# Gate and up projections of a decoder step on one NeuronCore: the normed tokens, the last splits and one weight sum in another place

## The chip, the cores and the metric

The kernel runs on one core of one Trainium2 chip. The metric is the device time of one execution in microseconds (us). Three runs of the kernel before took 882.13, 884.52 and 888.44 us, median 884.52. The profiled execution took 884.46 us.

## The reference, cut to what matters

One layer of a decoder for 512 prompt tokens and 8 sample tokens, width 1024. The part in question is its dense feed-forward network, in float32, at the end of the layer:

```python
hf = rmsnorm(x, g_ffn)
x = x + (jax.nn.silu(hf @ w_gate) * (hf @ w_up)) @ w_down      # 1024 -> 2816 -> 1024
```

Behind it only one more norm follows.

## The kernel before, in words

Tokens lie along the free dimension: all 520 of them, as two halves of `H2` = 260 columns, and features on the 128 partitions. Every float32 operand is split in two reduced parts, a rounded one (`hi`, a cast on ScalarE) and the rest (`lo`, a subtraction on VectorE, lines 191 and 192 for activations and Strassen weights, 208 and 209 for plain weights). A product is three matmuls: hi x hi, hi x lo, lo x hi.

**The feed-forward network** has 22 blocks `f` of 128 hidden features. The first four (`PLAIN`) are computed plainly: `proj` (line 223) multiplies the gate's weights and then the up weights with A, the split of the tokens with their gain but without the inverse norm `r_bc`; VectorE reads the PSUM (`pfg` at line 1194, `pfu` at 1200), multiplying by `r_bc`. PSUM for these has two buffers.

The other 18 blocks compute gate and up together by a Strassen-Winograd scheme: the 2 x 2 blocks are gate and up against the two halves of the features for the weights (a11, a12 in the raw tile `g`; a21, a22 in `u`), and the two halves of the features against the two halves of the tokens for the activations. Seven products `j` of 12 matmuls (84 for a block) replace eight. Three more weight operands, s1 = a21 + a22, s2 = s1 - a11, s4 = a12 - s2, and s3 = a11 - a21, are sums that VectorE makes (lines 1175 to 1178) for block f+1 while block f is multiplied; s3 and s1 share a tile, and these tiles have two buffers, the same that plain weights use. Raw weight tiles have three. The split weight operands (`qhi`, `qlo`) rotate through eight buffers.

The seven activation operands `xs` are made once. `operands()` multiplies X by gain and `r_bc` (line 1152, eight instructions, 'normed tokens'), forms four sums (1156 to 1164) and splits seven times. It is a generator: `spawn` puts it among the tasks and `step()` asks each task for its next piece. The results of products are read from PSUM at lines 1221 to 1232 in an order set by `j`; line 1234 writes the block's product to `FR`.

**The down projection** (line 1257) needs the 22 blocks split. Blocks 0 to 7 go to A during the Strassen stage (`ff_split`). Blocks 8 to 21 go to `TT`, where `xs` lies: products of the last block free it, two blocks' worth for each product. It takes the two PSUM buffers that `pfa` and `pfb` have had.

**The order of the work** on each engine is made when the program is built: a list scheduler with a model of the machine's times (`schedule_with_timeline_sim=True`) takes the instructions in the order in which the code issues them as priority and sets them as they come ready in its model. Each engine then works its list strictly in order. Weight loads are issued on SP's queue (`wraw`, line 199); POOL's queue issues nothing in this part of the kernel before.

Of the kernel before, what the change touches and what calls it, by code (L numbers as in the profile page):

```python
# [13 lines left out]
AF = mybir.ActivationFunctionType  # L14
# [9 lines left out]
P = 128  # L24
D = 1024
KB = 8
# [114 lines left out]
def decoder_step(ctx: ExitStack, tc: tile.TileContext, i: dict, o: list):  # L141
# [23 lines left out]
    def ps1(name):  # L165
        return psums[-1].tile([P, 512], F32, tag="msc", name=name)
# [30 lines left out]
    def wraw(at, n):  # L197
        raw = wp.tile([P, KB * P], F32, tag="wraw", name="wraw", bufs=3)
        sp.dma_start(raw[:, :n], i["weights"][at : at + P * n].rearrange("(p n) -> p n", p=P))
        return raw  # L200
# [29 lines left out]
    def spawn(gen, group=None):  # L230
        tasks.append([gen, 0, group])
# [914 lines left out]
    def xsplit(j, x):  # L1146
        split(*xs[j], x)

    def operands():

        for k in range(KB):
            dve.scalar_tensor_tensor(xn[:, :, k], halves(X[:, k]), vec[:, k, V_GF : V_GF + 1], r_h, ALU.mult, ALU.mult)
            if k % 2:
                yield 1
        b11, b21, b12, b22 = (xn[:, a, k : k + 4].rearrange("p k n -> p (k n)") for a in range(2) for k in (0, 4))
        t3 = fr[:, 12 * N : 14 * N]
        dve.tensor_tensor(t3, b22, b12, ALU.subtract)
        dve.tensor_tensor(b12, b12, b11, ALU.subtract)
        xsplit(0, b11)
        yield 1  # L1160
        dve.tensor_tensor(b11, b22, b12, ALU.subtract)
        xsplit(4, b21)
        yield 1
        dve.tensor_tensor(b21, b21, b11, ALU.subtract)
        for j, x in ((1, t3), (6, b22), (3, b12), (2, b11), (5, b21)):
            xsplit(j, x)
            yield 1

    def weight_operands(out):

        g, u = (wraw(W.next()[1], KB * P) for _ in range(2))
        yield 1
        s13, s24 = (wp.tile([P, KB * P], F32R, tag=t, name="wsum", bufs=2).bitcast(F32) for t in ("whi", "wlo"))
        a11, a12, a21, a22, s3, s1, s2, s4 = (t[:, z : z + 4 * P] for t in (g, u, s13, s24) for z in (0, 4 * P))
        dve.tensor_tensor(s3, a11, a21, ALU.subtract)  # L1175
        dve.tensor_tensor(s1, a21, a22, ALU.add)
        dve.tensor_tensor(s2, s1, a11, ALU.subtract)
        dve.tensor_tensor(s4, a12, s2, ALU.subtract)
        for w in (a11, s3, s2, s1, a12, a22, s4):
            hi, lo = (tp.tile([P, 4 * P], F32R, tag="q" + t, name="q" + t, bufs=8) for t in ("hi", "lo"))  # L1180
            split(hi, lo, w)
            out.append((hi, lo))
            yield 1

    def ff_split(f, raw):
        split(ff(0, f, slice(None)), ff(1, f, slice(None)), raw)

    spawn(operands())
    ops = []
    for f in range(PLAIN):  # L1190
        ps = proj(A, "pfg")
        gu = tp.tile([P, 4, H2], F32, tag="gu", name="gu").rearrange("p (a z) n -> p a (z n)", a=2)
        g, u = gu[:, 0], gu[:, 1]
        dve.tensor_tensor(halves(g), ps[:, :, :H2], r_h, ALU.mult)
        act.activation(g, g, AF.Silu)
        if f == PLAIN - 1:
            spawn(weight_operands(ops))
        step()
        ps = proj(A, "pfu", ahead=int(f < PLAIN - 1))
        dve.tensor_tensor(halves(u), ps[:, :, :H2], r_h, ALU.mult)  # L1200
        dve.tensor_tensor(FR[:, f], u, g, ALU.mult)
        step()
    drain()
    for f in range(PLAIN, FB):
        last, nxt = f == FB - 1, []
        more = weight_operands(nxt) if not last else iter(())
        next(more, None)
        ab, cd = ps2("pfa"), ps2("pfb")
        ps = [*(ps1(z)[:, :H2] for z in ("pfc", "pfd")), ab[:, 0, :H2], ab[:, 1, :H2], ps1("pfe")[:, :H2], cd[:, 0, :H2], cd[:, 1, :H2]]
        gu = tp.tile([P, 4, H2], F32, tag="gu", name="gu")  # L1210
        g1, g2, v1, v2 = (gu[:, z] for z in range(4))
        for j, (out, (wh, wl), (xh, xl)) in enumerate(zip(ps, ops, xs)):
            for k in range(4):
                for w, x in ((wh, xh), (wh, xl), (wl, xh)):
                    pe.matmul(  # L1215
                        out, w[:, k * P : (k + 1) * P], x[:, k * H2 : (k + 1) * H2],
                        start=k == 0 and w is wh and x is xh, stop=k == 3 and w is wl,
                    )
            next(more, None)
            if j == 0:  # L1220
                act.copy(g1, out)
            elif j == 2:
                dve.tensor_tensor(g2, out, g1, ALU.add)
                dve.tensor_tensor(v1, ps[1], g2, ALU.add)
            elif j == 3:
                dve.tensor_tensor(gu[:, 1::2], out.unsqueeze(1).broadcast_to([P, 2, H2]), gu[:, 1:3], ALU.add)  # L1226
            elif j == 4:
                dve.tensor_tensor(g1, out, g1, ALU.add)
                act.activation(g1, g1, AF.Silu)
            elif j == 6:  # L1230
                dve.tensor_tensor(gu[:, 1:3], cd[:, ::-1, :H2], gu[:, 1:3], ALU.add)
                act.activation(g2, g2, AF.Silu)
                to = FR[:, f - KB if f >= KB else f]
                dve.tensor_tensor(halves(to), gu[:, 0:2], gu[:, 2:4], ALU.mult)
            if f - PLAIN < KB and j == 5:
                ff_split(f - PLAIN, FR[:, f - PLAIN])
            if last:
                if j == 1:
                    W.fill(1)
                for z in (2 * j, 2 * j + 1):  # L1240
                    ff_split(KB + z, FR[:, z])
        list(more)
        ops = nxt
    tp_cm.__exit__(None, None, None)
# [4 lines left out]
    for obs in ((0, 1), *((ob,) for ob in range(2, KB - 1))):  # L1249
        pss = [ps2("pfd") for _ in obs]  # L1250
        for k0 in range(0, FB, KB):
            for ps in pss:
                hi, lo = W.get()
                for k in range(k0, min(k0 + KB, FB)):
                    for w, s in ((hi, 0), (hi, 1), (lo, 0)):
                        for a in range(2):
                            pe.matmul(  # L1257
                                ps[:, a, :H2], w[:, k - k0], ff(s, k, slice(a * H2, (a + 1) * H2)),
                                start=k == 0 and w is hi and s == 0, stop=k == FB - 1 and w is lo,
                            )  # L1260
        for ob, ps in zip(obs, pss):
            xb = X[:, ob]
            dve.tensor_tensor(halves(xb), halves(xb), ps[:, :, :H2], ALU.add)
            square(yp, ob)
            act.activation(xb, xb, AF.Copy, scale=vec[:, ob, V_GO : V_GO + 1])
# [106 lines left out]
```

## Time and profile before

| what | value |
|---|---|
| median of three runs | 884.52 us |
| the profiled execution | 884.46 us |
| its span on the core | 882.7 us |
| PE busy in the span | 838.9 us (95%) |
| mean granted TensorE clock | 0.983 |
| plain blocks of the feed-forward network | from 495 to 550 us |
| Strassen blocks | from 550 to 734 us |
| down projection | from 740 us |

The span is the time from the first to the last instruction; what lies around it is 1.8 us. PE is TensorE, DVE VectorE, ACT ScalarE, POOL GpSimd, SP the queue that issues loads. L1152 is line 1152 of the kernel. A wait is put down to the instruction that ended it.

### The profile page before, as it was taken

The page shows a single profiled execution, that of the slowest core. Times are in us where ns is not written, and L with a number is a line of the kernel's source. Part 1 is how long each engine was busy: PE and PEld are TensorE (multiplying, and loading weights), DVE is VectorE, ACT ScalarE, POOL GpSimd, SP SyncE. Part 2 cuts the span into 40 slices and gives each one's busy share as a digit, 9 for nine tenths or more (in the row PEclk, how much of TensorE's full clock was granted, in tenths as well). Part 3 has the DMA queues.
Part 4 walks back from the last instruction along what each step waited for, and adds up shares of the span by engine and source line. Part 5 has one row for each costly group of instructions (what it writes and reads, how often), then busy time and mean ns, then how long its engine had stood idle before and what let it go on. Part 6 is the DMA issues. An engine that isn't in the chain of part 4 may idle for free.

```text
span 882.7 us, 16987 instructions
## 1 busy us (share of the span) xinstructions
PE 838.9 (95%) x6707; PEld 821.9 (93%) x6707; DVE 673.3 (76%) x1509; ACT 397.4 (45%) x791; POOL 182.4 (21%) x188
## 2 busy tenths in 40 slices
PE   6999999999999999999999889999999997999994
PEld 5989989999999999889999879999999997999994
DVE  5899999877786678867888897999999997222224
ACT  5455435444546354355443554554445554222221
POOL 5544432221024301424323300000000000010011
PEclk9999999999999999999999989999999998999997
DMA  8333223334235336784764112223332232233213
GB/s 270 98 97 124 83 96 121 123 100 133 94 144 195 118 129 217 254 283 135 223 215 133 66 66 73 97 96 115 122 101 96 97 120 66 84 105 94 90 43 98
DMA packets 34600, 110.56 MB, mean 125 GB/s; under 512 B 4000, under 2 KB 8480, under 8 KB 34264
## 3 DMA queue, kind: packets, MB, share of 16 engines
q1 hardware_dynamic: 28752, 96.06, 33.9%
q0 software_dynamic: 3616, 12.34, 3.9%
q10 hardware_dynamic: 2152, 1.08, 0.5%
q8 instruction: 53, 0.87, 0.4%
q14 instruction: 27, 0.22, 0.1%
HBM read 100.38 MB, written 9.07 MB: 124 GB/s over the span
## 4 chain that ended last, share of the span: by engine, by line
PE 76%; DVE 15%; DMA 3%; issue 2%; ACT 2%; POOL 1%; SPq 0%; DVEq 0%; ACTq 0%; POOLq 0%
PE pfd L1257 13%; PE pfa L1215 6%; PE pfb L1215 6%; PE pcq L223 5%; PE pgt L223 4%; PE pwc L223 4%; PE ppl L223 4%; PE pfg L223 3%; PE pfc L1215 3%; PE pwo L223 3%; PE pfe L1215 3%; PE prp L223 3%; PE pfd L1215 3%; PE pfu L223 2%; DVE cv L518 2%
## 5 line engine op out<-in xcount | busy, mean ns | idle before, releaser
L208 ACT CAST whi<-wraw 128x1024 fp32r<-128x1024 f32 (+1 forms) x104 | 107.2, 1032 | 185.4 <-PE pfd L1257 69.6
L209 DVE TENSOR_TENSOR wlo<-wraw,whi 128x1024 fp32r<-128x1024 f32 (+1 forms) x85 | 108.9, 1282 | 74.9 <-ACT whi L208 72.9
L302 POOL TENSOR_TENSOR ssq<-ssq,sq 128x520 f32<-128x520 f32 x18 | 29.3, 1628 | 371.8 <-ACT sq L301 366.6
L191 ACT CAST qhi<-wsum 128x512 fp32r<-128x512 f32 x72 | 42.9, 619 | 54.1 <-DVE wsum L1175 45.7
L1257 PE MATMUL pfd<-TT,whi 128*128 128x260 f32 x392 | 62.8, 282 | 0.0
L209 POOL TENSOR_TENSOR wlo<-wraw,whi 128x1024 fp32r<-128x1024 f32 x19 | 46.0, 2419 | 67.7 <-ACT whi L208 62.6
L1215 PE MATMUL pfa<-TT,qhi 128*128 128x260 f32 x288 | 53.8, 284 | 0.0
L1257 PEld LDWEIGHTS pfd<-TT,whi 128*128 128x128 f32 x392 | 53.7, 188 | 0.0
L1215 PE MATMUL pfb<-TT,qhi 128*128 128x260 f32 x288 | 53.0, 283 | 0.0
L192 DVE TENSOR_TENSOR qlo<-wsum,qhi 128x512 fp32r<-128x512 f32 x72 | 47.9, 687 | 0.0
L223 PE MATMUL pwc<-B,whi 128*128 128x260 f32 x256 | 43.8, 287 | 3.6 <-DVE X L291 3.0
L223 PE MATMUL ppl<-A,whi 128*128 128x260 f32 x256 | 46.4, 295 | 0.6 <-DVE up L510 0.6
L223 PE MATMUL pcv<-A,whi 128*128 128x260 f32 x256 | 45.6, 294 | 1.1 <-ACT whi L208 1.1
L1215 PEld LDWEIGHTS pfb<-TT,qhi 128*128 128x128 f32 x288 | 44.5, 188 | 0.0
L1215 PEld LDWEIGHTS pfa<-TT,qhi 128*128 128x128 f32 x288 | 44.4, 188 | 0.0
L223 PE MATMUL pgt<-A,whi 128*128 128x260 f32 x256 | 44.0, 287 | 0.0
L223 PE MATMUL prp<-A,whi 128*128 128x260 f32 x256 | 43.8, 287 | 0.0
L1257 PE MATMUL pfd<-A,whi 128*128 128x260 f32 x224 | 37.3, 290 | 6.0 <-DVE gu L1226 6.0
L223 PE MATMUL pcq<-A,whi 128*128 128x260 f32 x256 | 42.0, 283 | 0.0
L1215 PE MATMUL pfa<-TT,qlo 128*128 128x260 f32 x144 | 40.9, 284 | 0.6 <-DVE qlo L192 0.6
L223 PE MATMUL pwo<-B,whi 128*128 128x260 f32 x256 | 41.3, 283 | 0.0
L1215 PE MATMUL pfb<-TT,qlo 128*128 128x260 f32 x144 | 40.8, 283 | 0.0
(435 smaller groups left out, 2625.4 us busy)
## 6 DMA issues: line engine op xcount, KB each, us to landing
wraw<-in_weights_dram SPq DMA_DIRECT2D x132, 512.0 KB, 3.7
kv<-in_cache_k_dram SPq DMA_DIRECT2D x16, 512.0 KB, 4.3
kv<-in_cache_v_dram SPq DMA_DIRECT2D x16, 512.0 KB, 4.3
wraw<-in_weights_dram SPq DMA_DIRECT2D x8, 384.0 KB, 3.1
X<-in_x_dram SPq DMA_DIRECT2D x2, 1040.0 KB, 6.0
Cs<-in_state_C_dram POOLq DMA_DIRECT2D x4, 512.0 KB, 5.1
out_dram<-Cs POOLq DMA_DIRECT2D x4, 512.0 KB, 3.4
Ss<-in_state_S_dram POOLq DMA_DIRECT2D x4, 512.0 KB, 3.9
```

The lines of the kernel that those rows point to most:

```text
L191: act.copy(hi, src)
L192: dve.tensor_tensor(lo, src, hi.bitcast(F32), ALU.subtract)
L208: act.copy(hi[:, :n], raw[:, :n])
L209: (pool if index in LO_ON_POOL else dve).tensor_tensor(lo[:, :n], raw[:, :n], hi[:, :n].bitcast(F32), ALU.subtract)
L223: pe.matmul(ps[:m, a, :H2], w[:, k, c0 : c0 + m], x[:, s, xk, a * H2 : (a + 1) * H2], start=first and w is hi and s == 0, stop=last and w ...
L302: (dve if ob == KB - 1 else pool).tensor_tensor(ssq, ssq, s, ALU.add)
L518: dve.scalar_tensor_tensor(cv[:, :LO], up[:, j : j + LO], wc(j), cv[:, :LO], ALU.mult, ALU.add)
L1215: pe.matmul(out, w[:, k * P : (k + 1) * P], x[:, k * H2 : (k + 1) * H2], start=k == 0 and w is wh and x is xh, stop=k == 3 and w is wl,)
L1257: pe.matmul(ps[:, a, :H2], w[:, k - k0], ff(s, k, slice(a * H2, (a + 1) * H2)), start=k == 0 and w is hi and s == 0, stop=k == FB - 1 and ...
```

## The change

Three edits. (1) `spawn(operands())` stands behind the issue of the first gate block's reading instead of ahead of the plain blocks. (2) The seven products come in another order (operands a11, a12, s3, s2, s1, a22, s4), PSUM readings are put together differently, and the splits of blocks 8 to 21 are asked for from the fifth product of the last block on, two per product, and then one per two steps of the down projection. (3) s1 isn't summed by VectorE: a21 is loaded a second time into the place of s1 by a plain DMA on SP's queue, and a22 is loaded onto it by a DMA on POOL's queue that adds.

```diff
@@ -1159,24 +1159,28 @@
         xsplit(0, b11)
         yield 1
         dve.tensor_tensor(b11, b22, b12, ALU.subtract)
-        xsplit(4, b21)
+        xsplit(1, b21)
         yield 1
         dve.tensor_tensor(b21, b21, b11, ALU.subtract)
-        for j, x in ((1, t3), (6, b22), (3, b12), (2, b11), (5, b21)):
+        for j, x in ((2, t3), (3, b11), (4, b12), (5, b21), (6, b22)):
             xsplit(j, x)
             yield 1
 
     def weight_operands(out):
 
-        g, u = (wraw(W.next()[1], KB * P) for _ in range(2))
-        yield 1
+        at, at_u = W.next()[1], W.next()[1]
+        g, u = wraw(at, KB * P), wraw(at_u, KB * P)
         s13, s24 = (wp.tile([P, KB * P], F32R, tag=t, name="wsum", bufs=2).bitcast(F32) for t in ("whi", "wlo"))
         a11, a12, a21, a22, s3, s1, s2, s4 = (t[:, z : z + 4 * P] for t in (g, u, s13, s24) for z in (0, 4 * P))
+        for z, op in ((0, ALU.bypass), (4 * P, ALU.add)):
+            (pool if z else sp).dma_start(
+                s1, i["weights"][at_u : at_u + P * KB * P].rearrange("(p n) -> p n", p=P)[:, z : z + 4 * P], accum_op=op
+            )
+        yield 1
         dve.tensor_tensor(s3, a11, a21, ALU.subtract)
-        dve.tensor_tensor(s1, a21, a22, ALU.add)
         dve.tensor_tensor(s2, s1, a11, ALU.subtract)
         dve.tensor_tensor(s4, a12, s2, ALU.subtract)
-        for w in (a11, s3, s2, s1, a12, a22, s4):
+        for w in (a11, a12, s3, s2, s1, a22, s4):
             hi, lo = (tp.tile([P, 4 * P], F32R, tag="q" + t, name="q" + t, bufs=8) for t in ("hi", "lo"))
             split(hi, lo, w)
             out.append((hi, lo))
@@ -1185,7 +1189,13 @@
     def ff_split(f, raw):
         split(ff(0, f, slice(None)), ff(1, f, slice(None)), raw)
 
-    spawn(operands())
+    unsplit = list(range(KB, FB))
+
+    def rest_split(n):
+        for _ in range(min(n, len(unsplit))):
+            f = unsplit.pop(0)
+            ff_split(f, FR[:, f - KB])
+
     ops = []
     for f in range(PLAIN):
         ps = proj(A, "pfg")
@@ -1193,6 +1203,8 @@
         g, u = gu[:, 0], gu[:, 1]
         dve.tensor_tensor(halves(g), ps[:, :, :H2], r_h, ALU.mult)
         act.activation(g, g, AF.Silu)
+        if f == 0:
+            spawn(operands())
         if f == PLAIN - 1:
             spawn(weight_operands(ops))
         step()
@@ -1206,7 +1218,8 @@
         more = weight_operands(nxt) if not last else iter(())
         next(more, None)
         ab, cd = ps2("pfa"), ps2("pfb")
-        ps = [*(ps1(z)[:, :H2] for z in ("pfc", "pfd")), ab[:, 0, :H2], ab[:, 1, :H2], ps1("pfe")[:, :H2], cd[:, 0, :H2], cd[:, 1, :H2]]
+        pc, pd, pe_ = (ps1(z)[:, :H2] for z in ("pfc", "pfd", "pfe"))
+        ps = [pc, pd, ab[:, 0, :H2], ab[:, 1, :H2], pe_, cd[:, 0, :H2], cd[:, 1, :H2]]
         gu = tp.tile([P, 4, H2], F32, tag="gu", name="gu")
         g1, g2, v1, v2 = (gu[:, z] for z in range(4))
         for j, (out, (wh, wl), (xh, xl)) in enumerate(zip(ps, ops, xs)):
@@ -1218,15 +1231,15 @@
                     )
             next(more, None)
             if j == 0:
-                act.copy(g1, out)
-            elif j == 2:
-                dve.tensor_tensor(g2, out, g1, ALU.add)
-                dve.tensor_tensor(v1, ps[1], g2, ALU.add)
+                act.copy(g2, out)
+            elif j == 1:
+                dve.tensor_tensor(g1, out, g2, ALU.add)
+                act.activation(g1, g1, AF.Silu)
             elif j == 3:
+                dve.tensor_tensor(g2, out, g2, ALU.add)
+                dve.tensor_tensor(v1, ps[2], g2, ALU.add)
+            elif j == 4:
                 dve.tensor_tensor(gu[:, 1::2], out.unsqueeze(1).broadcast_to([P, 2, H2]), gu[:, 1:3], ALU.add)
-            elif j == 4:
-                dve.tensor_tensor(g1, out, g1, ALU.add)
-                act.activation(g1, g1, AF.Silu)
             elif j == 6:
                 dve.tensor_tensor(gu[:, 1:3], cd[:, ::-1, :H2], gu[:, 1:3], ALU.add)
                 act.activation(g2, g2, AF.Silu)
@@ -1235,10 +1248,10 @@
             if f - PLAIN < KB and j == 5:
                 ff_split(f - PLAIN, FR[:, f - PLAIN])
             if last:
-                if j == 1:
+                if j == 3:
                     W.fill(1)
-                for z in (2 * j, 2 * j + 1):
-                    ff_split(KB + z, FR[:, z])
+                if j > 3:
+                    rest_split(2)
         list(more)
         ops = nxt
     tp_cm.__exit__(None, None, None)
@@ -1258,6 +1271,8 @@
                                 ps[:, a, :H2], w[:, k - k0], ff(s, k, slice(a * H2, (a + 1) * H2)),
                                 start=k == 0 and w is hi and s == 0, stop=k == FB - 1 and w is lo,
                             )
+                    if k % 2:
+                        rest_split(1)
         for ob, ps in zip(obs, pss):
             xb = X[:, ob]
             dve.tensor_tensor(halves(xb), halves(xb), ps[:, :, :H2], ALU.add)
```

In the listings that follow, names stand as in the code: `FR` and `X` hold tokens, `gu` the readings, `TT` the split operands and later the split blocks.

VectorE where the plain blocks begin; a leading minus marks rows of before alone, a plus rows of the change alone:

```order
 L278 SCALAR_TENSOR_TENSOR r_bc<-r_bc,nrml 128x260 x2
-L1152 SCALAR_TENSOR_TENSOR FR<-X,vec,r_bc 128x2x260 x6
-L1194 TENSOR_TENSOR gu<-pfg,r_bc 128x520
-L1152 SCALAR_TENSOR_TENSOR FR<-X,vec,r_bc 128x2x260 x2
-L1200 TENSOR_TENSOR gu<-pfu,r_bc 128x520
+L1204 TENSOR_TENSOR gu<-pfg,r_bc 128x520
+L1152 SCALAR_TENSOR_TENSOR FR<-X,vec,r_bc 128x2x260 x8
+L1212 TENSOR_TENSOR gu<-pfu,r_bc 128x520
 L209 TENSOR_TENSOR wlo<-wraw,whi 128x1024
 L192 TENSOR_TENSOR TT<-FR,TT 128x1040
```

The reading of the first gate block moved ahead of all eight instructions for the normed tokens; the reading of the first up block and a weight split stay behind them.

VectorE of the change in one of the last Strassen blocks, with numbers that tell buffers apart: `wsum_8790`, `wsum_8928` and `wsum_9066` are the tiles of s3 and s1 of three blocks that follow each other (the third uses the first one's buffer):

```order
L192 TENSOR_TENSOR qlo_8885<-wsum_8790,qhi_8884 128x512
L1240 TENSOR_TENSOR gu_8799<-pfa_8794,gu_8799 128x260
L192 TENSOR_TENSOR qlo_8902<-wraw_8788,qhi_8901 128x512
L1242 TENSOR_TENSOR gu_8799<-pfe_8798,gu_8799 128x2x260
L192 TENSOR_TENSOR qlo_8918<-wsum_8791,qhi_8917 128x512
L1244 TENSOR_TENSOR gu_8799<-pfb_8795,gu_8799 128x520
L192 TENSOR_TENSOR qlo_8954<-wraw_8924,qhi_8953 128x512
L1247 TENSOR_TENSOR FR_6315<-gu_8799 128x520
L192 TENSOR_TENSOR qlo_8971<-wraw_8924,qhi_8970 128x512
L1181 TENSOR_TENSOR wsum_9067<-wsum_9066,wraw_9062 128x512
L1236 TENSOR_TENSOR gu_8937<-pfd_8935,gu_8937 128x260
L192 TENSOR_TENSOR qlo_8989<-wsum_8928,qhi_8988 128x512
```

The first row is the split of s1 of one block, which frees its buffer; L1181 reads the s1 that the two loads have put there for the block after next, eight rows later. In before no row of VectorE waits for a load of s1; its sum stood at line 1176.

VectorE of the change in the last block:

```order
L1236 TENSOR_TENSOR gu<-pfd,gu 128x260
L192 TENSOR_TENSOR TT<-FR,TT 128x520 x3
L1239 TENSOR_TENSOR gu<-pfa,gu 128x260
L192 TENSOR_TENSOR TT<-FR,TT 128x520
L1240 TENSOR_TENSOR gu<-pfa,gu 128x260
L192 TENSOR_TENSOR TT<-FR,TT 128x520 x2
L1242 TENSOR_TENSOR gu<-pfe,gu 128x2x260
L192 TENSOR_TENSOR TT<-FR,TT 128x520 x4
L1244 TENSOR_TENSOR gu<-pfb,gu 128x520
```

In before, eight splits and the readings of `pfd` and `pfe` stood between the block's first reading of `pfa` (L1223) and its second one (L1226), and three of the splits directly ahead of that; now both readings of `pfa` follow that of `pfd` with three splits and one split between.

## Rows read from the trace of the kernel before

**Rows 1.** The page, part 1: busy us (share of span) x instructions.

```profile
PE 838.9 (95%) x6707; PEld 821.9 (93%) x6707; DVE 673.3 (76%) x1509; ACT 397.4 (45%) x791; POOL 182.4 (21%) x188
```

**Rows 2.** Stages: length, busy us per engine, granted clock, DMA share, GB/s.

```profile
495.00:498.50 3.50, 3.50 (x19) 3.50 (x18) 3.50 (x4) 3.03 (x5) 3.12 (x2) 0.54 0.02 5
...
509.00:513.40 4.40, 0.01 (x1) 0.02 (x1) 4.40 (x8) 1.97 (x3) 0.00 (x0) 0.83 0.00 1
513.40:518.70 5.30, 5.29 (x24) 5.30 (x25) 5.30 (x7) 3.79 (x5) 0.00 (x0) 0.50 0.22 79
...
553.00:720.00 167.00, 167.00 (x1389) 166.98 (x1388) 159.32 (x283) 82.55 (x165) 0.00 (x0) 1.00 0.32 107
...
734.50:740.50 6.00, 0.01 (x1) 0.00 (x0) 5.97 (x11) 1.30 (x3) 0.00 (x0) 0.72 0.19 66
740.50:744.30 3.80, 3.77 (x18) 3.80 (x19) 2.02 (x3) 2.33 (x3) 0.00 (x0) 0.54 0.02 4
744.30:760.00 15.70, 15.70 (x133) 15.70 (x132) 2.45 (x2) 2.72 (x3) 0.00 (x0) 1.00 0.20 59
```

**Rows 3.** PE's waits from 480 us on: in total us, times, longest.

```profile
PE pfd L1257 <- DVE gu L1226: 6.0, 1, 6.0
PE pfg L223 <- DVE gu L1194: 4.4, 1, 4.4
PE pwc L223 <- DVE X L291: 3.0, 2, 2.7
...
PE pfa L1215 <- DVE qlo L192: 0.6, 1, 0.6
PE pfe L1215 <- ACT qhi L191: 0.5, 1, 0.5
```

**Rows 4.** VectorE in order of time, first gate and up block: start, us.

```profile
508.55 4.11 DVE L1152 SCALAR_TENSOR_TENSOR FR<-X,vec,r_bc 128x520 f32<-128x520 f32 x6
512.58 0.69 DVE L1194 TENSOR_TENSOR gu<-pfg,r_bc 128x520 f32<-128x520 f32 x1
513.18 1.42 DVE L1152 SCALAR_TENSOR_TENSOR FR<-X,vec,r_bc 128x520 f32<-128x520 f32 x2
```

**Rows 5.** PE in order of time at the same place.

```profile
513.41 1.21 PE L223 MATMUL pfg<-A,whi 128*128 128x260 f32 x4 [4.41 <-DVE gu L1194]
```

**Rows 6.** VectorE in order of time, end of the last block.

```profile
737.19 0.43 DVE L1224 TENSOR_TENSOR gu<-pfd,gu 128x260 f32<-128x260 f32 x1
737.52 0.42 DVE L1228 TENSOR_TENSOR gu<-pfe,gu 128x260 f32<-128x260 f32 x1
737.86 1.92 DVE L192 TENSOR_TENSOR TT<-FR,TT 128x520 fp32r<-128x520 f32 x3
739.69 0.70 DVE L1226 TENSOR_TENSOR gu<-pfa,gu 128x520 f32<-128x520 f32 x1
```

**Rows 7.** VectorE's groups in the Strassen stage: x count | busy, mean ns.

```profile
L1176 DVE TENSOR_TENSOR wsum<-wraw 128x512 f32<-128x512 f32 x16 | 11.0, 685 | 0.0
```

**Rows 8.** VectorE in order of time, one block inside that stage.

```profile
694.04 1.28 DVE L192 TENSOR_TENSOR qlo<-wsum,qhi 128x512 fp32r<-128x512 f32 x2
```

**Rows 9.** DMA issues of the whole run: KB each, median us from issue to landing.

```profile
wraw<-in_weights_dram SPq DMA_DIRECT2D x132, 512.0 KB, 3.7
...
wraw<-in_weights_dram SPq DMA_DIRECT2D x8, 384.0 KB, 3.1
...
Cs<-in_state_C_dram POOLq DMA_DIRECT2D x4, 512.0 KB, 5.1
...
Ss<-in_state_S_dram POOLq DMA_DIRECT2D x4, 512.0 KB, 3.9
...
mraw<-in_mem_dram POOLq DMA_DIRECT2D x2, 512.0 KB, 7.0
...
cosr<-in_rope_dram POOLq DMA_DIRECT2D x1, 260.0 KB, 2.9
```

**Rows 10.** The same view of 560 to 720 us alone.

```profile
wraw<-in_weights_dram SPq DMA_DIRECT2D x32, 512.0 KB, 4.3
```

## The prediction

> **What bounds the kernel now.** I read busy shares first, then stages, then what the busiest engine waits for. PE is busy 95% of the span [rows 1]. In the table of stages [rows 2] the Strassen stage (553 to 720 us) has PE at 167.00 of 167 us at full granted clock, with VectorE at 159.32: nothing done for another engine can gain there while PE stays full; it can only cost. So the gain must lie at the two edges. Before it, 509 to 513.4 us, PE does nothing and VectorE all the time; behind it, 734.5 to 740.5 us, the same. After each gap the granted clock is about half for a while. PE's waits [rows 3] name four: 4.4 us on the reading of the first gate block, 6.0 us on a reading of the last block, 0.6 and 0.5 us on splits. The profiled execution took 884.46 us around a span of 882.7 us, as good as the median of 884.52; the sum is made against 884.46.
>
> **The start.** VectorE has the inverse norms at 508.55 us and then forms six normed token blocks before it reads the gate block [rows 4]; PE, which has two PSUM buffers there, stands until that reading ends [rows 5]. In the change the reading comes first and all eight follow. It then ends at 508.55 + 0.69 = 509.2; from a reading's end to PE's start the rows show 513.41 - (512.58 + 0.69) = 0.14 us, so PE starts at 509.4 instead of 513.41: 4.0 us saved. The 24 matmuls behind the gap took 5.30 us at clock 0.50 (the 1.2 GHz level); at full clock one costs 167.00 / 1389 = 0.120 us, so 2.9 us: 2.4 saved if the clock stays up. Against that: the eight normed blocks (4.11 + 1.42 us) now stand ahead of the reading of the first up block and of the split of the weights of the second up block. PE reaches that block at 509.4 + 48 x 0.120 = 515.2; the reading is over at 509.2 + 5.4 + 0.6 = 515.2, just in time, but the split ends at 516.3 where PE wants it four matmuls in, at 515.7: 0.6 to 0.7 us lost. Net 5.7 us. Some matmuls of the first Strassen block now stand inside the plain ones; moving them is free by the same addition: the buffer of their weights is free at 527.3 us (the split of the third up block), a load lands 3.7 to 4.3 us later [rows 9, 10], the cast adds 0.6, which is 532.2 at the latest, and PE arrives at 533.2.
>
> **The end.** In the last block VectorE has three splits directly ahead of the reading of pfa [rows 6]; PE needs that PSUM for the down projection and waits 6.02 us. In the change VectorE's order from the end of product pfd on is: its reading, three splits, a reading of pfa, one split, the other reading of pfa; that is 3 x 0.34 + 4 x 0.6 = 3.4 us, while PE has five more products (60 x 0.120 = 7.2 us) before the down projection. So I cost this wait at nothing: 6.0 saved. 18 matmuls then took 3.80 us at clock 0.54 instead of 2.2: 1.6. The waits of 0.6 and 0.5 us inside the block come from splits queued ahead of its operands [rows 3, 6], which now come later: 1.1. The splits moved into the down projection are hidden: VectorE is busy 2.45 of 15.7 us there [rows 2], and their readers come after 16 steps of six matmuls, 11.5 us. Sum 8.7 us; both edges 14.4.
>
> **The adding loads.** Removed: one VectorE sum of 128x512 per block, 18 in all. A run of two such operations costs 1.28 us, so 0.6 each in a row [rows 7, 8]: VectorE has some 11 us less, all beside PE, worth nothing by itself. The different order of the readings is worth nothing either, with the same six per block. Added per block: a plain 256 KB load on SP's queue and a 256 KB adding one on POOL's, which waits for the first. POOL has no other work there. The order table shows the new chain: the buffer of block k's sum is free when its split is done; then plain load, then adding load, then VectorE's L1181 of block k+2, and VectorE runs in order, so from there everything waits for it, among it the next block's split of its sum. One pass of this loop is c (both loads with their hand-overs) plus VectorE's work from L1181 to that split. I counted that work over the 16 steps with 0.6 us per 512-column operation and reading, 0.34 per 260-column one (737.19 to 737.52 in [rows 6]): it runs from 0 to 5.2 us, 4.3 in each of the last three, 51.0 in all. PE needs 84 x 0.120 = 10.1 us a block, 161.6 for 16. The loop holds PE up once 16 c + 51.0 > 161.6: **from c = 6.9 us on, 16 us for each further us.** Short lags are covered by VectorE's lead; I give no credit for it.
>
> No trace shows an adding load. The plain load: 384 KB take 3.1 us and 512 KB 3.7 [rows 9], thus 2.5 to 3.0 for 256 KB, I take 2.8. The adding one: at least a plain POOL load of its size, 2.9 (260 KB, cosr); at most the slowest POOL load of 512 KB, 7.0. To add, the old 256 KB must be fetched besides the new, so the nearest rows are POOL's loads of 512 KB: 3.9 and 5.1; I take 3.9, since here nothing else is on POOL. Three hand-overs of 0.14 make 0.4. c = 2.8 + 3.9 + 0.4 = 7.1 us: 16 x 7.1 + 51.0 - 161.6 = 3.0 us lost. With the ends 2.5 + 2.9 and 3.0 + 7.0 c is 5.8 (no loss) to 10.4 (56 us).
>
> The Trainium skill (DMA: Bandwidth & Descriptors, Anatomy of one DMA) prices a POOL load at 2.0 us plus bytes by 436 GB/s: an estimate of 2.6 us for 256 KB and 3.2 for twice that, so c of 5.6 to 6.2 and no loss; the rows, 2.9 for 260 KB and 3.9 for 512 KB, stand above it. The same page (Rules for kernel authors) says that an accumulating load reads its destination and writes it later, and needs a wait for the earlier load; no run here shows it yet, and it speaks for the doubled bytes.
>
> **Forecast.** 884.46 - 14.4 + 3.0 = **873 us**, chance 0.46; its own range 870 to 876.
>
> **Rivals.**
> *The loads are cheap* (0.10): c stays under 6.9, as the 2.9 us of cosr allow; nothing is lost and 870 us result. For it: POOL's queue is empty. Against: the table's larger loads. The skill's formula above is this rival's rule.
>
> *The loads share the engines* (0.20): two weight loads per block go on beside them. 512 KB take 4.3 us in this stage against 3.7 over the whole run [rows 9, 10]; 0.6 us more on one of the two gives c = 7.7, 12.6 us lost, 882.7 us, no change. That the queues of SP, ACT and POOL end in the same 16 engines is also what the skill states (the same page, Issuing engines are not separate DMA queues).
>
> *Slower: the adding load sets the pace* (0.16): it takes 5.1 us, as the POOL loads of Cs do, and the plain one 3.4. Then c = 8.9, 16 x 8.9 + 51.0 - 161.6 = 31.8 us lost, 902 us; PE would wait 2 us in every block, on splits behind L1181. The point where the gain is eaten is c = 6.9 + 14.4/16 = 7.8. For it: POOL loads of 512 KB spread from 3.9 to 7.0 us. Against: those ran beside POOL's own work.
>
> *The edges give less* (0.08): the waits go but the clock falls all the same (it was 0.54 at 495 us too, behind a wait of 2.7 us [rows 2, 3]), or the last readings wait for a weight split put ahead of them; 4 us less, 877 us. That the change does not do what it says I exclude: the order shows the reading ahead of all normed tokens, 18 adding loads, and each reading between splits.
>
> **Numbers.** A measurement tells about 1%, 8.8 us, from no change. Faster by more (under 875.7) needs c under 7.3 with full edges: the forecast but a tail, and the cheap loads, 0.54. Same: the shared engines, less gain, the tail, 0.29. Slower: 0.17. The range 868 to 893 leaves out the slow adding load and a thin end below.
>
> **What would show it.** The start: PE's idle time before the second gate block under 0.5 us, clock 1.00 behind it, and a wait of some 0.7 us in the second up block. The end: no wait of the first pfd on VectorE. The loop: landing time of the wsum loads, 2.8 and 3.9 us, and VectorE's idle time before L1181; if that sums to more than some 10 us and PE has idle time in 553 to 720 us, the loop binds. Wrong would be: an adding load over 5 us, or new PE waits on the casts of the first Strassen block.

## The result, and the profile after

The changed kernel takes **905.99 us** (median of four runs, 903.52 to 909.44) where the kernel before takes 885.43 beside it: ratio 1.024, 95% interval 1.0205 to 1.0274. It is slower, by about 20 us; the forecast was 873, its range 868 to 893. The profiled execution took 909.44 us around a span of 907.6; it is the slowest of the four, so the table below, made of profiled executions, shows a loss of 24.9 us where the medians show 20.6.

Three stretches of PE's work tell where the time is. They run from the first gate matmul to the first down matmul (gate and up), from there to the last down matmul, and from that to the end of the span. The third kernel is the best of the experiments (e14); its profiled execution is the fastest of its six, and 4.0 us of its lead lie ahead of the first gate matmul, where nothing was changed.

| | before | changed | e14 |
|---|---|---|---|
| first gate matmul starts, us | 495.05 | 494.02 | 491.05 |
| gate and up, us | 245.5 | 265.4 | 234.3 |
| down products, us | 129.0 | 127.5 | 127.5 |
| behind the last down matmul, us | 13.1 | 20.7 | 13.5 |

So the changed kernel lost 19.9 us in gate and up and 7.6 behind the last matmul, and won 1.5 in the down products; 1.0 us lies ahead of everything that was changed.

**The start went as predicted.** The first two fences are VectorE and PE of the changed kernel in order of time, to be held against [rows 4] and [rows 5] (start, us, and in brackets the wait); the third is the table of stages that answers to [rows 2].

```profile
507.59 0.70 DVE L1204 TENSOR_TENSOR gu<-pfg,r_bc 128x520 f32<-128x520 f32 x1
508.21 5.45 DVE L1152 SCALAR_TENSOR_TENSOR FR<-X,vec,r_bc 128x520 f32<-128x520 f32 x8
```

```profile
508.44 0.71 PE L223 MATMUL pfg<-A,whi 128*128 128x260 f32 x4 [0.38 <-DVE gu L1204]
```

```profile
509.00:513.40 4.40, 4.40 (x39) 4.40 (x38) 4.40 (x7) 2.91 (x3) 0.00 (x0) 1.00 0.00 0
513.40:518.70 5.30, 4.98 (x40) 4.62 (x39) 5.30 (x7) 3.94 (x4) 0.00 (x0) 1.00 0.34 99
```

The wait is 0.38 us instead of 4.41, and the granted clock stays at 1.00 where it was 0.83 and 0.50. **The wait at the end went too.** The first down matmul waits 0.87 us, not 6.0 [rows 3]; what took it away is the subject of e10:

```profile
759.39 0.75 PE L1270 MATMUL pfd<-A,whi 128*128 128x260 f32 x4 [0.87 <-DVE gu L1240]
```

**Between the edges PE is now held up.** First PE's waits from 545 to 755 us (total, times, longest), then the same stretch in the table of stages:

```profile
PE pfa L1228 <- DVE gu L1240: 15.5, 9, 3.2
PE pfb L1228 <- DVE gu L1244: 1.8, 1, 1.8
PE pfc L1228 <- ACT gu L1234: 1.7, 1, 1.7
PE pfc L1228 <- DVE qlo L192: 1.1, 2, 0.9
PE pfa L1228 <- ACT qhi L191: 0.2, 1, 0.2
```

```profile
545.00:755.00 210.00, 189.70 (x1478) 186.16 (x1477) 162.68 (x288) 94.57 (x187) 14.83 (x17) 0.96 0.51 137
```

The waits sum to 20.3 us, which is the idle time of that row (210 - 189.70). And 1478 matmuls at 0.120 us would be 177.4 us, not 189.70. Of these 12 us some 8 are the clock, which falls after several of the waits (0.96 in the mean, and 0.04 x 210 = 8.4); the rest is not taken apart. PE waits for VectorE's readings of PSUM, but VectorE itself waits for the weight sum. Line L1181 (min, median and max ns, first and last start) and what its engine sat idle for (us, times), then the two loads of the sum (KB, median us to landing), then one block's loads and L1181 on SP, POOL and VectorE:

```profile
L1181 DVE TENSOR_TENSOR wsum<-wsum,wraw x18: 684/693/695, 547.2 to 736.1; 128x512 f32<-128x512 f32 x18
...
  DMA wsum<-in_weights_dram: 45.5, 15
```

```profile
wsum<-in_weights_dram SPq DMA_DIRECT2D x18, 256.0 KB, 2.7
wsum<-in_weights_dram POOLq DMA_DIRECT2D x18, 256.0 KB, 4.8
```

```profile
716.67 0.33 SPq L1176 DMA_DIRECT2D wsum<-in_weights_dram  x1
...
728.62 0.33 SPq L1176 DMA_DIRECT2D wsum<-in_weights_dram  x1
```

```profile
719.89 0.87 POOL L1176 DMA_DIRECT2D wsum<-in_weights_dram  x1 [11.63 <-DVE gu L1244]
```

```profile
724.21 0.69 DVE L1181 TENSOR_TENSOR wsum<-wsum,wraw 128x512 f32<-128x512 f32 x1 [3.01 <-DMA wsum<-in_weights_dram]
```

One pass of the loop can be read off: plain load issued at 716.67, adding load 3.2 us later, L1181 4.3 us behind that, and 4.4 us of VectorE's work until the next plain load goes out at 728.62: 11.95 us for a block of which PE needs 10.1. (What ended POOL's wait is, by the code, the landing of the plain load, 0.56 us ahead, and not the VectorE reading that the bracket names.) Over the last 16 blocks the two loads took 8.72 us in the mean (3.63 from issue to issue, 5.09 from the adding load's issue to L1181) and VectorE's work 2.60; the sum, 11.32, is the mean distance of two L1181, by the way it is counted.

**Behind the last matmul stands what the prediction did not have.** ScalarE at the end of the last block, and then in the last 26 us:

```profile
755.24 1.28 ACT L1258 ACT_TABLE_LOAD   x1
756.53 0.63 ACT L191 CAST TT<-FR 128x520 fp32r<-128x520 f32 x1
757.18 1.28 ACT L1237 ACT_TABLE_LOAD   x1
758.48 0.42 ACT L1237 ACTIVATE gu<-gu 128x260 f32<-128x260 f32 x1
...
882.37 1.28 ACT L273 ACT_TABLE_LOAD   x1 [2.47 <-PE pn L1292]
...
884.16 1.28 ACT L275 ACT_TABLE_LOAD   x1
...
891.59 1.28 ACT L273 ACT_TABLE_LOAD   x1
892.88 0.37 ACT L273 ACTIVATE nrml<-pn,vec 128x130 f32<-128x130 f32 x1
893.27 1.28 ACT L275 ACT_TABLE_LOAD   x1
...
894.89 1.28 ACT L273 ACT_TABLE_LOAD   x1
...
896.57 1.28 ACT L275 ACT_TABLE_LOAD   x1
```

The same place of the kernel before, where one load, behind the last Silu, serves all that follows:

```profile
742.99 1.28 ACT L1245 ACT_TABLE_LOAD   x1
...
871.60 0.35 ACT L273 ACTIVATE nrml<-pn,vec 128x130 f32<-128x130 f32 x1
871.98 0.31 ACT L275 ACTIVATE nrml<-nrml 128x130 f32<-128x130 f32 x1
872.20 0.35 ACT L273 ACTIVATE nrml<-pn,vec 128x130 f32<-128x130 f32 x1
872.58 0.31 ACT L275 ACTIVATE nrml<-nrml 128x130 f32<-128x130 f32 x1
```

The set of logarithm and exponential is asked for by a line that is pinned behind the ScalarE instruction written just ahead of it. Before, that was the split of the last block's own result, which cannot run before the last Silu. The change writes the split of an older block there, whose data lie ready; so the set is loaded at 755.24, ahead of the last block's two Silu, the Silu at 758.48 fetches its own set back, and at the end logarithm and exponential fetch a set for each call: six loads of 1.28 us. Four of them stand one behind the other on the last chain (5.1 us). The two at 882.37 and 884.16, for the first half of the tokens, hold up VectorE, so that the square of the last tokens starts 3.6 us behind the last down matmul instead of 1.0 (2.5 us); together that is the 7.6 us of the table. That logarithm and exponential can share one set is what the Trainium skill states (ScalarE: Activation LUTs, Table sets: the hidden batching unit); the trace of before agrees, in which the four calls follow each other without a load. The same page (What ACT_TABLE_LOAD costs) adds a drain of 1.38 us to each switch; no such gap is seen here (a load ends at 892.87, the next ACTIVATE starts at 892.88).

### The profile page after: what moved, and what is told of

The parts are those of the page before. It is cut to its first block, busy times and chain, and to the rows that moved or that the text cites. A ratio compares the mean times of both kernels' runs of the same rounds, so it can differ in the third digit from the quotient of the medians.

```text
span 907.6 us, 17189 instructions
## 1 busy us (share of the span) xinstructions
PE 846.2 (93%) x6707; PEld 825.6 (91%) x6707; DVE 662.1 (73%) x1491; ACT 406.9 (45%) x798; POOL 198.2 (22%) x206
## 4 chain that ended last, share of the span: by engine, by line
PE 58%; DVE 20%; DMA 12%; issue 5%; ACT 3%; POOL 1%; SPq 0%; DVEq 0%; POOLq 0%; ACTq 0%
PE pfd L1270 12%; DMA wsum<-in_weights_dram 7%; PE pcq L223 5%; PE pgt L223 4%; PE ppl L223 3%; PE pwc L223 3%; PE pwo L223 3%; PE prp L223 3%; PE pfa L1228 3%; PE pfb L1228 3%; DVE qlo L192 2%; PE pfg L223 2%; DVE wlo L209 2%; DVE cv L518 2%; PE pfu L223 1%
## 5 line engine op out<-in xcount | busy, mean ns | idle before, releaser
L1228 PE MATMUL pfa<-TT,qhi 128*128 128x260 f32 x288 | 58.5, 303 | 15.7 <-DVE gu L1240 15.5
L1228 PEld LDWEIGHTS pfa<-TT,qhi 128*128 128x128 f32 x288 | 48.3, 205 | 17.8 <-DVE gu L1240 6.7
L1176 POOL DMA_DIRECT2D wsum<-in_weights_dram x18 | 15.8, 876 | 219.7 <-DVE gu L1244 45.1
L1181 DVE TENSOR_TENSOR wsum<-wsum,wraw 128x512 f32<-128x512 f32 x18 | 12.5, 692 | 47.6 <-DMA wsum<-in_weights_dram 45.5
L1228 PE MATMUL pfa<-TT,qlo 128*128 128x260 f32 x144 | 42.8, 297 | 0.0
```

Source lines behind the costliest of these rows:

```text
L1176: (pool if z else sp).dma_start(s1, i["weights"][at_u : at_u + P * KB * P].rearrange("(p n) -> p n", p=P)[:, z : z + 4 * P], accum_op=op)
L1228: pe.matmul(out, w[:, k * P : (k + 1) * P], x[:, k * H2 : (k + 1) * H2], start=k == 0 and w is wh and x is xh, stop=k == 3 and w is wl,)
```

## The experiments

Ratios are against the kernel before, in the same group of runs, with 95% intervals.

**The table set (e1), the sum given back to VectorE (e2), both (e3), the loads alone (e4).**

```diff
 e1, on the changed kernel
                 act.activation(g2, g2, AF.Silu)
+                if last:
+                    tc.keep_in_program_order(act.preload_act_table_set(LOG_EXP))
...
     tp_cm.__exit__(None, None, None)
-    tc.keep_in_program_order(act.preload_act_table_set(LOG_EXP))
 e2, on the changed kernel
-        for z, op in ((0, ALU.bypass), (4 * P, ALU.add)):
-            (pool if z else sp).dma_start(
...
+        dve.tensor_tensor(s1, a21, a22, ALU.add)
         dve.tensor_tensor(s2, s1, a11, ALU.subtract)
```

e1: 

> The changed kernel with one thing moved: the load of the log/exp table set stands right behind the last Silu instead of behind the last split that is written. Theory (table set): in the changed kernel that load slid ahead of the last block's two Silu, which brought their own set back, so that six set loads of 1.28 us stand in the last 25 us of the program, and from the last down matmul to the end it takes 20.6 us instead of 13.0. Then this kernel has one such load behind the last Silu, 13 us behind the last down matmul and about 898.4 us in all (906.0 less 7.6). Rival (the end is long for another reason, the clock or the output's transfers): 906 within 2 us.

e2: 

> The changed kernel without its adding loads: VectorE adds the weight halves again as in the kernel before; the two moves of splits and the new order of products stay. Theory (loads): the weight loads cost all of the loss in the middle of the gate and up stage, about 33 us, so 873 to 878 us (884.5 less 14.4 for the two edges, plus up to 7.6 while the table set is loaded too early). Rival (the new order of products and of the VectorE's PSUM reads holds TensorE): PE still waits 10 us or more for VectorE between 560 and 740, and the time stays above 890.

e3 (e1 and e2 together): 

> Both: VectorE adds, and the table set is loaded behind the last Silu. Loads and table set: 870 us (884.5 less 14.4), 7 to 8 us under the kernel with the sum alone. If the table set is off the path: the same as that kernel within 2 us. If the order of products is the loss: above 885.

e4 (the loads written into the kernel before): 

> The kernel before with the adding loads alone: old order of splits and of products, last splits where they were. Theory (loads, in any order of the products): about 33 us slower than before, 912 to 920. Rival 1 (the loop of loads as the prediction had it, with 4.8 instead of 3.9 us for the adding load, 8.0 us in all): 17 us slower, 902. Rival 2 (only in the new order does the wait stand ahead of PSUM reads): within 5 us of before.

Measured: e1 909.14 us (1.0284, 1.0243 to 1.0325); e2 881.32 (0.9964, 0.9943 to 0.9985); e3 874.75 (0.9879, 0.9834 to 0.9925); e4 901.91 (1.0205, 1.0162 to 1.0248).

e2 settles the main point: without the adding loads, and with everything else of the change, PE waits between the edges for 2.4 us in the last block and for little else (0.2 us), and 25 us of the 906 are gone. The view is that of PE's waits again:

```profile
PE pfb L1225 <- DVE gu L1241: 2.4, 1, 2.4
```

Still e2 lies 3.3 us above the range expected of it, and e3 4.8 us above its 870: the edges give less than 14.4. e3 against e2 prices the table set: 6.6 us, and the stretch behind the last matmul is 13.3 us instead of 21.2. e4 came out at rival 1's 902, so the loads cost in either order of the products. But its own loop is short: the two loads take 8.57 us, VectorE's work 1.96, and L1181 stand 10.52 us apart, which over 16 blocks is 6.7 us more than PE's 10.1. Gate and up is 14.8 us longer than before, and 10.5 of that lie between the last L1181 and the first down matmul; PE's waits from 545 to 750 us, most of them on readings of pfa, sum to 12.1 us. The hit is in the figure, not in the whole of its reasoning. e1 missed its 898: its end is 13.6 us long, as expected, but its gate and up stage is 270.9 us. I come back to that with e13.

**Is it the adding (e5), is it the loop (e6, e9)?** Three kernels on top of e1.

```diff
 e5
-        for z, op in ((0, ALU.bypass), (4 * P, ALU.add)):
+        for z, op in ((0, ALU.bypass), (4 * P, ALU.bypass)):
 e6
...
+        n = next(blocks)
+        if n > 1:
+            s1 = FR[:, 8 + n % 6, : 4 * P]
         for z, op in ((0, ALU.bypass), (4 * P, ALU.add)):
-            (pool if z else sp).dma_start(
+            tc.keep_in_program_order((pool if z else sp).dma_start(
...
 e9, on e6
-        g, u = wraw(at, KB * P), wraw(at_u, KB * P)
         s13, s24 = (...)
...
         for z, op in ((0, ALU.bypass), (4 * P, ALU.add)):
...
+        g, u = wraw(at, KB * P), wraw(at_u, KB * P)
```

e5: 

> The changed kernel with the table set behind the last Silu, whose second load of each block overwrites the weight sum instead of adding to it (the sum is then one half of the weights, and the outputs are another function): same loads, same bytes, same waits, without the adding. Theory (loop of two tiles: both loads, then VectorE's work up to the split that frees the tile, 8.7 + 2.6 = 11.3 us a block against 10.1 of TensorE): a plain second load lands about 1.9 us sooner, the loop takes 9.4 us, TensorE's 10.1 us decide again, and only the later first operand is left of the loss: 880 us, 878 to 886. Rival (the two more loads a block cost by sharing the DMA engines with the weights, or by a wait ahead of PSUM reads whatever its length): above 895.

e6: 

> The changed kernel with the table set behind the last Silu and, from the third block on, the weight sum in six places that are free in the token buffer, so that the first load waits for no split; it is issued right behind the load of its up weights. The adding loads stay. Theory (loop of two tiles): with the loop open the loads' 8.7 us lie beside TensorE's work, and what is left is the later first operand: 883 us, 879 to 888. Rival (the adding load's length itself, or the new order of products, holds TensorE): above 895, VectorE still waiting 2 us or more a block for the sum.

e9: 

> The kernel with the six places in the token buffer, and both loads of the sum now asked for ahead of the block's gate and up loads instead of behind them. In the kernel with the places alone the loop had only closed elsewhere: the up load waited in SP's queue until s4, which stands behind the wait for the sum, had read the gate tile (L1187 ends at 664.74, base load 665.20), and a block took 11.4 us as before. Theory (what costs is a loop through the two loads, whichever tile closes it): now the first load goes out about a block earlier, VectorE no longer waits for the sum, a block takes TensorE's 10.1 us, and the time is 877 to 886. Rival (long adding loads or the new order of products hold TensorE without a loop): above 893, VectorE still waiting 1 us or more a block for the sum.

Measured: e5 886.59 us (1.0031, 1.0005 to 1.0056); e6 901.66 (1.0198, 1.0161 to 1.0236); e9 884.93 (1.0012, 0.9988 to 1.0037).

e5: a plain second load lands in 3.6 us where the adding one takes 4.8. The two lines are the loads of e5; the third is what VectorE sat idle for ahead of L1181:

```profile
wsum<-in_weights_dram SPq DMA_DIRECT2D x18, 256.0 KB, 2.8
wsum<-in_weights_dram POOLq DMA_DIRECT2D x18, 256.0 KB, 3.6
```

```profile
  DMA wsum<-in_weights_dram: 26.1, 15
```

The loop is 7.36 + 2.70 = 10.06 us, the distance of two L1181 is 10.06, and 21 to 23 us of the time of e1 and e13 are gone. The estimate was 1.9 us for the adding, it is 1.2. e5 came out 6.6 us above what I expected: with the loop as long as its own block PE still waits 11.3 us from 545 to 745 us, 3.2 of them ahead of the down products.

e6 failed, and told more than a hit would have. The sum had six places and its first load waited for no split, and still VectorE waited for the sum in each block. VectorE, then SP, in order of time:

```profile
662.51 0.69 DVE L1186 TENSOR_TENSOR wsum<-FR,wraw 128x512 f32<-128x512 f32 x1 [2.53 <-DMA FR<-in_weights_dram]
...
664.06 0.68 DVE L1187 TENSOR_TENSOR wsum<-wraw,wsum 128x512 f32<-128x512 f32 x1
```

```profile
664.82 0.33 SPq L199 DMA_DIRECT2D wraw<-in_weights_dram  x1
665.20 0.42 SPq L1181 DMA_DIRECT2D FR<-in_weights_dram  x1
```

L1187 (s4) is the last reader of a weight tile; when it ends, at 664.74, SP's next weight load may go, and the sum's first load stands behind that in SP's queue. The loop had closed through another tile: 8.84 + 2.54 = 11.38 us a block. In e9 the sum's loads stand ahead of the block's weight loads, and PE is idle for only 2.5 us of 168 (573 to 741 us):

```profile
573.00:741.00 168.00, 165.45 (x1368) 164.70 (x1367) 148.95 (x264) 88.97 (x174) 12.23 (x14) 1.00 0.57 152
```

1368 matmuls in 165.45 us are 0.121 us each, at full clock, though the adding loads are all there. So it is neither the adding itself nor the new order of products that holds PE, but a loop that is longer than PE's block. In that stretch VectorE still sits idle 3.2 us ahead of L1187 for the sum and 11.2 for weights that are now asked for later, nearly all of it off PE's path. e9 lacks 10 us to e3. PE's waits from 545 to 746 us sum to 9.9 us in e9 (3.1 at 567.6 us, 4.1 ahead of the down products) and to 3.7 in e3; the rest is not taken apart.

**Which edge brings what (e8, e10, e11, e14).** On the kernel before: e8 has the first edit alone; e10 has the late splits of the second edit, but the old order of products and readings, with the table set placed as in e1; e11 has both. e14 is e3 again, with more executions.

```diff
 e8
-    spawn(operands())
...
         act.activation(g, g, AF.Silu)
+        if f == 0:
+            spawn(operands())
 e10
             if last:
...
-                for z in (2 * j, 2 * j + 1):
-                    ff_split(KB + z, FR[:, z])
+                if j > 3:
+                    rest_split(2)
...
+                    if k % 2:
+                        rest_split(1)
```

e8: 

> The kernel before with the first edit alone: the normed tokens are asked for behind the first plain block's reading. Theory (the start edge as the prediction has it): 5.7 us less than before, 879.4. Rival (the wait only moves to a later split of the tokens): within 2 us of before.

e10: 

> The kernel before with the second edit alone (last splits behind the last block's readings), and the table set loaded behind the last Silu. Theory (the end edge as the prediction has it): 8.7 us less than before, 875.2 to 876.4. Rival (splits that are now made beside the down products hold TensorE there): within 3 us of before, with waits for TT in the down products.

e11: 

> The kernel before with both edges, the table set behind the last Silu, the old order of products and VectorE's own sum. Theory (the two edges add up, the new order of products has no part in them): 884.5 less 14.4, 870, within 3 us of the kernel with the new order and the sum (874.75). Rival (the new order is needed for the end edge): 878 or more.

e14: 

> The changed kernel with VectorE's sum and the table set behind the last Silu, again: 874.75 us within 2, some 7 us under the kernel with both edges in the old order of products (881.8), if the new order of products is what lets the last block's readings stand ahead of the splits.

Measured: e8 881.07 us (0.9966, 0.9939 to 0.9993); e10 885.06 (1.0005, 0.9979 to 1.0031); e11 881.78 (0.9948, 0.9926 to 0.9970); e14 **872.50** (0.9853, 0.9823 to 0.9884).

e10 is the surprise: the late splits alone give nothing. VectorE and PE at the end of its last block:

```profile
736.69 0.42 DVE L1231 TENSOR_TENSOR gu<-pfd,gu 128x260 f32<-128x260 f32 x1
737.03 0.42 DVE L1235 TENSOR_TENSOR gu<-pfe,gu 128x260 f32<-128x260 f32 x1
737.37 1.91 DVE L192 TENSOR_TENSOR TT<-FR,TT 128x520 fp32r<-128x520 f32 x3
739.19 0.69 DVE L1233 TENSOR_TENSOR gu<-pfa,gu 128x520 f32<-128x520 f32 x1
```

```profile
740.03 0.77 PE L1265 MATMUL pfd<-A,whi 128*128 128x260 f32 x2 [6.03 <-DVE gu L1233]
```

That is [rows 6] again, three splits and all, although the splits are written further back. The reading of pfa that PE needs (L1233) adds to what L1230 and L1231 have read before it, so it comes third in a row, and splits fill in between; and one of the two products into pfa is PE's last of all, from 732.4 to 734.0. The reading ends at 739.9, 5.9 us after that. In e14 both products into pfa are done at 717.5, ahead of both into pfb, and the reading that takes the place (L1237) adds only to what L1236, the other reading of pfa, has made. Splits stand ahead of it too, but it ends at 725.3, and PE, whose last product ends at 724.9, goes on nearly at once:

```profile
721.60 0.42 DVE L1236 TENSOR_TENSOR gu<-pfa,gu 128x260 f32<-128x260 f32 x1
721.94 1.91 DVE L192 TENSOR_TENSOR TT<-FR,TT 128x520 fp32r<-128x520 f32 x3
723.77 1.22 DVE L209 TENSOR_TENSOR wlo<-wraw,whi 128x1024 fp32r<-128x1024 f32 x1
724.90 0.42 DVE L1237 TENSOR_TENSOR gu<-pfa,gu 128x260 f32<-128x260 f32 x1
```

```profile
721.83 0.48 PE L1225 MATMUL pfb<-TT,qhi 128*128 128x260 f32 x2 [3.02 <-DVE gu L1241]
...
725.38 0.39 PE L1268 MATMUL pfd<-A,whi 128*128 128x260 f32 x1 [0.44 <-DVE gu L1237]
```

The first of these two rows is the price: inside the last block PE now waits 3.0 us for a reading of pfb, ahead of which moved splits stand in VectorE's queue. So the end edge is the work of the new order of products and readings; whether in it the earlier products or the shorter chain of readings counts is not shown, no run changes one alone, and none has the new order without the late splits. e11 against e14 shows it in the time: 881.8 and 872.5 us. e14 beats both kernels, the one before by 1.5%; it is the change without its third part, with the table set put where it belongs.

**The changed kernel again (e7, e12), and beside it the moved table set (e13).** e7 and e12 are the changed kernel, e13 is e1, unchanged.

e7: 

> The changed kernel once more, beside the kernels of this group. If the kernel with the table set moved was no faster (909 for 906) because the loads landed later in those runs (9.05 against 8.72 us for both loads together): this one is 3 to 10 us slower than 906. If the move of the table set itself costs in the middle what it gains at the end: 906 within 3 us, under the 909.

e12: 

> The changed kernel, as the reference of this group: 906 to 909 us. Its end, from the last down matmul, is 20.7 us with the set loads, whatever the chip.

e13: 

> The changed kernel with the table set behind the last Silu, again. If the move only helps, and the group of runs made the earlier difference: 7 us under the changed kernel of this group. If the splits that it lets in ahead of the last block's PSUM reads on VectorE (five and three between the readings, where three and one stood) give the gain back: within 3 us of it, with a wait of 3 us ahead of the first down matmul and a down projection of 130 us instead of 127.5.

Measured: e7 907.57 us (1.0282, 1.0242 to 1.0322); e12 909.55 (1.0285, 1.0250 to 1.0319); e13 907.58 (1.0250, 1.0226 to 1.0275). e7 is within 3 us of the first 906, as the second of its cases has it. e13 is within 2 us of e12: its end is 13.0 us instead of 21.7, its gate and up stage 268.3 instead of 262.7. Part of that is the splits. With the set load moved, VectorE's order has more of them ahead of the last readings of pfa. In e13:

```profile
758.12 3.13 DVE L192 TENSOR_TENSOR TT<-FR,TT 128x520 fp32r<-128x520 f32 x5
761.17 0.42 DVE L1239 TENSOR_TENSOR gu<-pfa,gu 128x260 f32<-128x260 f32 x1
761.50 1.91 DVE L192 TENSOR_TENSOR TT<-FR,TT 128x520 fp32r<-128x520 f32 x3
763.33 0.42 DVE L1240 TENSOR_TENSOR gu<-pfa,gu 128x260 f32<-128x260 f32 x1
```

where the changed kernel had three splits and one (756.14 and 758.31 us); the first down matmul waits 2.99 us, against 0.85 in e12; the down products stayed at 127.5 us, not the 130 of the second case. The loads took 8.91 us in e13 and 8.52 in e12, which over 16 blocks is 6 us; whether that difference belongs to the kernel or to the run is open. With the loop in place the move of the set is worth nothing that can be told; without it (e2, e3) 6.6 us.

## Why the prediction was wrong, step by step

Two steps failed, and they are what parts 873 from 906: in the loop of the adding loads the time c of both loads was put at 7.1 us and measured 8.72, mainly because the adding load took 4.8 us and not 3.9; and the table set of ScalarE had no term at all (6.6 us).

- **Start edge, 5.7 us: right.** From the first gate matmul to the last up matmul it was 55.3 us; it is 51.0 in the changed kernel, with ten matmuls of the first products, 1.2 us, moved in: 5.5 us. In e3 it is 49.5, but 1.4 us of that gain lie in the first 48 matmuls, ahead of what was changed: there the clock was near half for a while in before (0.54 in [rows 2]) and in the changed kernel, and 1.00 in e3. The wait in the second up block came, 0.32 us instead of 0.7. Alone (e8) the edit moved the median by only 2.8 us, with a wait of 1.0 us on a weight split that the changed kernel does not have.
- **End edge, 8.7 us: the wait and the clock came, the cause was not seen, and a new wait was put at nothing.** From the last product matmul to the first down matmul it was 6.3 us and is 0.7 in e3, and the down products take 1.5 less: 7.1 of the 7.6 forecast for the two. Of the waits of 0.6 and 0.5 us inside the block 0.2 are left, but one of 3.0 us on a reading of pfb, behind moved splits, came in their place. And I wrote that the different order of the readings was worth nothing; e10 and e11 show that the moved splits without it leave waits of 6.0 and 4.7 us.
- **Both edges, 14.4 us:** e3 and e14 give 10.4 and 13.6 us in the medians (12.7 in the profiles, 1.4 of it the clock named above).
- **Loop of the adding loads: the mechanism was right, one term was mis-sized, and it decided.** I took c = 2.8 + 3.9 + 0.4 = 7.1. Measured: 8.72 in the mean. In the 12 of these 16 passes of which the trace has both landings the plain load took 3.1 us (median 2.7), the adding one 4.8 and the hand-overs 0.6, so most of the error is the adding load's 0.9. With "16 us for each further us" as the slope, an error of 1.6 us in c is 26 us in the sum. The prediction's own formula with 8.72 gives 28.9 us of loss; the changed kernel's gate and up stage is 30.7 us longer than e2's. That they are so near is partly luck: VectorE's work in the loop was 2.60 us a block where 51.0 us over 16 blocks, 3.2 each, was counted, and 16 blocks of 11.32 us are only 19.5 us more than PE's 161.6. Against e3 the 31.0 us lie so: first L1181 8.3 us later, 15.9 more from the first to the last, 6.9 more from the last to the first down matmul. The sum had nothing for the first and the last of these.
- **The estimate by the Trainium skill's formula** (DMA: Bandwidth & Descriptors, Anatomy of one DMA) in the prediction, c of 5.6 to 6.2, takes the formula for POOL's loads also for the plain load on SP; with that load at 2.8 us it is 5.8 to 6.4, and the measured 8.72 lies above either.
- **The slow rival** (adding load 5.1, c = 8.9, 902 us, chance 0.16) was the one that came true, but for the place: PE waits mostly on readings of pfa that stand behind L1181 on VectorE (15.5 of 20.3 us) and hardly on splits (1.1).
- **Table set, 6.6 to 7.6 us: missing.** Of ScalarE the prediction has only casts; the set load, which the change lets run ahead of two Silu, is nowhere in it.

In sum: 885.4 less some 12 for the edges, plus 25 to 28 for the adding loads (e2 against the three medians of the changed kernel), plus 6.6 for the set, is 905 to 908.

## What to carry to other kernels

A load that starts when its own tile comes free is in a loop; its pass is latencies plus the work until the release, and it must be held against the bottleneck's time per block with a margin for every hand-over, because each error counts once per block. To open such a loop, look for every queue and tile by which it can close, not only for its own buffers. Moving other work behind a reading in the text does not put the reading first (e10); here it came early only together with an earlier product (e14). And when the last instruction that a pin refers to changes, see what the pin still holds.

## What the runs showed of the hardware

An adding load of 256 KB on POOL's queue took 4.8 to 5.0 us in the median in the changed kernel (e7 and e12 with it), e1, e4 and e13; a plain one in the same place took 3.6 (e5), a plain one on SP's queue 2.7 to 3.0. With the sum in the token buffer (e6, e9) it was 4.3 for the adding load and 4.0 to 4.5 for the plain one on SP. The Trainium skill's formula (DMA: Bandwidth & Descriptors, Anatomy of one DMA) gives an estimate of 2.6 us for 256 KB on POOL; the run with the plain load shows 1.0 us more. That an accumulating load reads its destination and writes it later (the same page, Rules for kernel authors) agrees with the 1.2 us between the two loads, though no run shows that reading by itself. Each switch of ScalarE's table set cost 1.28 us and no gap around it. The issue of an adding load holds POOL for 0.87 us, that of a plain one 0.54 (e5), which is 0.33 of the 1.2; an issue holds SP for 0.33 (0.42 into the token buffer). From the landing of the plain load to POOL's issue it was 0.56 us in each pass.
